# One two-layer hybrid block on one core: where the first output projection's bias is added, and when the convolution's taps are dealt

## Chip, cores and metric

The kernel runs on one core of one Trainium2 chip. The metric is the device time of one execution in microseconds (us), from launch to end on that core. Three executions of the kernel before gave 811.22, 810.73 and 818.46 us; the median is 811.22 us.

## What is computed

256 latent rows and 256 context rows of width 1024 go through two layers. Each layer has a mixer and a mixture of experts, and both are modulated by vectors that come from a conditioning input through a large matrix (`ada_w`, `ada_b`). The change touches the first layer's mixer only:

```python
m = jnp.split(silu_c @ ada_w[0] + ada_b[0], 6, axis=-1)          # one set for latent rows, one for context rows
u = h * (1 + m[1]) + m[0]
a, q, k, v = split(u @ w_in + b_in)
conv = silu(layer_norm(depthwise_conv(glu(a), conv_w, conv_b)))   # 31 taps, 512 channels
na   = attention(q, k, v)                                         # 8 heads; context rows and windowed latent rows
o    = concat([conv, na]) @ w_out + b_out
h    = layer_norm(alpha * h + m[2] * o)
```

So the row that is normalised is alpha·h + m2·(cat·w_out + b_out). After it come routing and the experts of layer 1, then the second layer.

## The kernel before

All weights stream from HBM through one list (`stream`) of 1 MB chunks. `pump` issues the next chunk on SyncE's queue (SP) whenever a buffer is free. There are four steady buffers (`w0` to `w3`); large scratch areas `x0` to `x4` are added to the free list by `lend` when the work that lives in them is over. The expert chunks of which the kernel knows the number ahead of routing are limited to 12 (`KNOWN0`). The order on every engine is the order in which the Python code emits instructions.

Products are made of three matmuls in float32r (`mm3`, lines 408 to 413): high part by high part, and the two mixed parts. Each weight chunk is therefore split into a high and a low part (lines 390 and 391, ScalarE and VectorE, or GpSimd where `low` is set; lines 401 and 402 do it piecewise on GpSimd during attention).

The stages of the first mixer, in order:

- `load_consts` (line 438 on): ScalarE's queue loads constants and, through `load_adab` (line 463), the modulation's bias: eight DMAs for each call, one for each of four column blocks and two conditioning vectors. `ada_done` (line 491) issues two more such calls on SP's queue.
- `inproj0` (line 581): ten chunks of the input projection. After each chunk some modulation matmuls (`self.ada(ADA_IN[c])`, line 482), then the evacuation of the chunk (lines 640, 641, 649, 651), then the split of a later chunk, then `self.bg(TAPS_IN[c])`. That last call emits convolution taps, which are VectorE instructions of 128x512 (line 632; the first of each channel block is line 630). There are 124 taps and four statistics steps in one queue, `bgq`.
- `attn0` (line 755) with `attend`: 32 jobs (a head and 128 query rows each) in a software pipeline over `i`. Scores on TensorE (line 786), maximum on VectorE (699), exponential on ScalarE (705), reciprocal on VectorE (713), scaling on GpSimd (714), transposes on TensorE (721), copy on ScalarE (723), product with v on TensorE (730), copies into the high and low operand of the next stage on ScalarE (577) and VectorE (578). A `hook(i)` after each step emits pieces of the output weight's split, `self.bg(TAPS_AT[i])`, the steps of the convolution's layer norm (`CONV_AT`), and modulation matmuls.
- `outproj` (line 861), called from `mix0` (line 2238): the output projection, four row tiles t of 128 rows, two column halves h of 512. First both weight groups of half 0 (`n` = 0, 1; attention rows first), into four PSUM banks `mm`; then half 1, tile by tile. There are four banks named `mm` in rotation. `end(t, h, ps)` multiplies a bank by m2 (line 2296, in `add_rows`), adds the residual row (line 878), and takes statistics (882); for h = 1 it also normalises the row. For layer 0 `forward` transposes the normalised row (569, 1126, 1128) and `back` computes routing logits (987) and transposes back through two more `mm` banks (1141).
- During `n` = 0 the hook in `mix0` emits the last four steps of the convolution's branch (lines 845 to 847, 574, 575), broadcasts m2 to all partitions (538, 533), multiplies it by the broadcast bias into `mb` (GpSimd, line 2273, four of 128x512) and turns the residual rows into alpha·x + mb (VectorE, line 2276, four of 128x1024). The bias row `bo` is loaded just before on ScalarE's queue (line 2253) into area 3, beside a zeroed tile that clears 4 MB in DRAM (line 2257).

Area 2 holds the attention's probabilities, area 3 the relative-position bias and later `bo` and the zeros, areas 0 and 1 the split of the last output weight, area 4 the convolution. Before, area 2 is lent at the end of `attn0`; areas 4 and 3 at `n` = 1, t = 0; areas 0 and 1 at the end.

Of the kernel before, what the change touches and what calls it, by code (L numbers as in the profile page):

```python
# [11 lines left out]
F32 = mybir.dt.float32  # L12
# [19 lines left out]

TAPS_IN = [9, 10, 10, 11, 12, 12, 12, 12, 14, 10]
TAPS_AT = [i % 2 for i in range(32)]

# [236 lines left out]
class Kern:  # L272
# [134 lines left out]

    def mm3(self, out, a, b, start, stop):
        (ah, al), (bh, bl) = a, b
        t = self.nc.tensor  # L410
        t.matmul(out, ah, bh, start=start, stop=False)  # L411
        t.matmul(out, ah, bl, start=False, stop=False)  # L412
        t.matmul(out, al, bh, start=False, stop=stop)  # L413

# [23 lines left out]
    def load_consts(self):  # L438
# [24 lines left out]
    def load_adab(self, l, g0, g1, at, eng):  # L463
        for j in range(4):
            src = self.d["ada_b"][l:l + 1].rearrange("o (g j n) -> o g j n", g=3, j=4)[:, g0:g1, j, :]
            for c in range(2):
                r = slice(32 * j + c, 32 * j + c + 1)
                if at == 4:
                    eng.dma_start(self.adar[4][r, :], src[:, 0])
                else:  # L470
                    eng.dma_start(self.adat[r, at:at + g1 - g0], src)

# [107 lines left out]

    def inproj0(self, M):
        nc, d, W = self.nc, self.d, self.W
# [171 lines left out]

    def attn0(self, M, qT, kT, v, acc):
        nc, d, W = self.nc, self.d, self.W
# [46 lines left out]
        def hook(i):  # L803
# [7 lines left out]
            if i % 2 == 1 and i // 2 < 16:  # L811
                self.ada(ADA_AT[i // 2])


# [40 lines left out]
        assert not self.bgq  # L855
        self.lend(self.end0 + 2, 2)

        return cath, catl, ln


    def outproj(self, l, cath, catl, tiles, order, base, hook=None):

        nc, T = self.nc, len(tiles)
        st, ends = {}, {}

        def prod(p, t, g, w, ks, start, stop):
            col = tiles[t][0]
            for k in ks:
                kt, sl = 4 * g + k, slice(k * 512, k * 512 + 512)
                self.mm3(p, (cath[:, kt, col:col + 128], catl[:, kt, col:col + 128]), (w[0][:, sl], w[1][:, sl]),  # L870
                         start and k == 0, stop and k == 3)

        def end(t, h, ps):
# [3 lines left out]
            yield  # L877
            nc.vector.tensor_tensor(s, s, o, op=OP.add)
            yield
# [1358 lines left out]
    def mix0(self):  # L2238
        nc, d, V = self.nc, self.d, self.nc.vector
        with self.phase("m0") as M:  # L2240
            with self.phase("m0i"):
                a = self.inproj0(M)
            with self.phase("m0a"):
                cath, catl, ln = self.attn0(M, *a)
# [4 lines left out]
                mb = M.tile([128, 4, 512], F32, name="v").rearrange("p (c h) n -> p c (h n)", c=2)  # L2249
                bo = self.area(3, [2, 1024])  # L2250
                bo, zero = bo[:, 0], bo[:, 1]
                nc.gpsimd.memset(zero, 0.0)
                nc.scalar.dma_start(bo, bass.AP(tensor=d["bo"].tensor, offset=d["bo"].offset, ap=[[0, 128], [1, 1024]]))

# [4 lines left out]
                def hook(n, t):  # L2259
                    if n == 0:  # L2260
                        next(ln)
                    if n == 1 and t == 0:
                        self.lend(self.end0, 4)
                        self.lend(self.end0 + 2, 3)
                    if n == 2 and t == 1:
                        self.ada_flush()
                    t -= 1
                    if n == 0 and t in (0, 1):
                        for h in range(2):
                            self.bcast_mod(m2[:, t], 1, 0, t, self.tp if h else None, halves=(h,))  # L2270
                        for h in range(2):
                            s = slice(h * 512, h * 512 + 512)
                            nc.gpsimd.tensor_tensor(mb[:, t, s], m2[:, t, s], bo[:, s], op=OP.mult)
                        for r in (2 * t, 2 * t + 1):
                            x = self.nt(r)
                            V.scalar_tensor_tensor(x, x, ALPHA, mb[:, t], op0=OP.mult, op1=OP.add)

                return self.outproj(0, cath, catl, TILES0, (1, 0, 0, 1),
                                    self.add_rows([m2[:, 0], m2[:, 1]], ("pT", 4)), hook)

# [286 lines left out]
```

## Time and profile before

| what | value |
|---|---|
| median of three runs | 811.22 us |
| the profiled execution's own time | 809.93 us |
| its span, first to last instruction | 808.1 us |
| TensorE busy (matmuls) | 711.7 us, 88% |
| VectorE busy | 475.1 us, 59% |
| ScalarE busy | 275.0 us, 34% |
| GpSimd busy | 236.8 us, 29% |
| mean granted TensorE clock | 0.944 |

How to read the rows below. A row of the timeline is: start, duration (us), engine, source line, operation, output <- input, shape, count; in brackets the idle time of that engine just before, and what released it. PE is TensorE, DVE VectorE, ACT ScalarE, POOL GpSimd; a q behind a name is that engine's queue of DMA issues. Rows of the same line in a row are merged, and the duration is then that of the whole run. A row of the windows view is: the stretch, its length, the busy time of PE, PEld (weight loads), DVE, ACT, POOL with counts, then the TensorE clock that was granted (1 is full), the busy share of the DMA engines, and GB/s. Busy shares are means over stages with different limits, so the argument goes by stage.

### The profile page before, as it was taken

How to read it: one execution, taken by the hardware profiler on the slowest of the kernel's cores; microseconds unless marked ns; L12 is line 12 of the kernel's file. 1: busy time of each engine (PE TensorE's matmuls, PEld its weight loads, DVE VectorE, ACT ScalarE, POOL GpSimd, SP SyncE). 2: the span in 40 equal slices, each digit the busy share in tenths (PEclk: the TensorE clock that was granted, in tenths of full speed). 3: DMA queues.
4: the chain of work that ended last, by engine and by line, in shares of the span. 5: the costliest groups of instructions: out<-in, count | busy, mean ns of one | idle time of the engine just before them, and what ended most of it. 6: DMA issues, size and time to landing. Idle time of an engine off the chain costs nothing. (4 is left out here: it accounts for less than half of the span.)

```text
span 808.1 us, 11464 instructions
## 1 busy us (share of the span) xinstructions
PE 711.7 (88%) x4162; PEld 417.9 (52%) x4162; DVE 475.1 (59%) x1004; ACT 275.0 (34%) x603; POOL 236.8 (29%) x254
## 2 busy tenths in 40 slices
PE   3799999949988987999999768969999987899993
PEld 0477777714566764434433337857556754454431
DVE  0578787866756878723334188397676388332115
ACT  0531222125756144201100127445677533121121
POOL 1200000026634012663000084163386450111111
PEclk9699999969999997999999978999999997899997
DMA  9974656447467528999997931637655494996892
GB/s 358 375 266 157 260 209 254 166 193 238 166 208 287 208 110 304 389 350 364 415 393 323 391 131 53 208 125 285 268 167 199 166 371 160 423 372 248 352 373 93
DMA packets 36269, 209.66 MB, mean 259 GB/s; under 512 B 4455, under 2 KB 4711, under 8 KB 15072
## 3 DMA queue, kind: packets, MB, share of 16 engines
q1 hardware_dynamic: 27872, 183.55, 58.8%
q10 hardware_dynamic: 4848, 13.86, 5.2%
q0 software_dynamic: 3472, 11.31, 3.7%
q8 instruction: 37, 0.61, 0.3%
q14 instruction: 40, 0.33, 0.1%
HBM read 197.92 MB, written 12.06 MB: 260 GB/s over the span
## 5 line engine op out<-in xcount | busy, mean ns | idle before, releaser
L632 DVE SCALAR_TENSOR_TENSOR x<-x,sm,x 128x512 f32<-128x512 f32 x120 | 90.7, 755 | 3.5
L411 PE MATMUL mm<-H,wh 128*128 128x512 f32 (+1 forms) x208 | 78.5, 377 | 1.8 <-ACT H L615 1.8
L413 PE MATMUL mm<-H,wl 128*128 128x512 f32 (+1 forms) x208 | 76.3, 367 | 0.7 <-DVE wl L391 0.7
L412 PE MATMUL mm<-L,wh 128*128 128x512 f32 (+1 forms) x208 | 76.5, 368 | 0.0
L482 PE MATMUL aux<-w,sc 128*32 128x512 f32 x368 | 52.2, 658 | 25.1 <-issue 9.2
L391 DVE TENSOR_TENSOR wl<-w,wh 128x512 fp32r<-128x512 f32 (+1 forms) x27 | 43.5, 1646 | 24.4 <-ACT wh L390 24.3
L401 POOL TENSOR_SCALAR wh<-w 128x256 fp32r<-128x256 f32 x32 | 13.7, 428 | 117.4 <-DMA w<-wo 117.3
L411 PEld LDWEIGHTS mm<-H,wh 128*128 128x128 f32 x208 | 40.3, 194 | 13.7 <-issue 2.5
L699 DVE TENSOR_REDUCE mx<-mm 128x1 f32<-128x512 f32 (+1 forms) x64 | 39.2, 616 | 13.2 <-PE mm L786 7.2
L1805 POOL TENSOR_TENSOR yl<-ada,yh 128x512 fp32r<-128x512 f32 x12 | 15.3, 1275 | 106.9 <-ACT yh L1802 106.9
L413 PEld LDWEIGHTS mm<-H,wl 128*128 128x128 f32 x208 | 40.3, 194 | 7.9 <-DVE wl L391 1.3
L412 PEld LDWEIGHTS mm<-L,wh 128*128 128x128 f32 x208 | 40.3, 194 | 7.1 <-DVE L L618 0.6
L411 PE MATMUL mm<-wh,H 128*128 128x512 f32 x104 | 42.8, 411 | 0.0
L723 ACT COPY pT<-tp 128x512 f32<-128x512 f32 (+1 forms) x64 | 33.9, 530 | 24.3 <-PE tp L721 24.0
L412 PE MATMUL mm<-wl,H 128*128 128x512 f32 x104 | 41.4, 398 | 0.0
L1382 PE MATMUL aux<-x,H 128*32 128x512 f32 (+2 forms) x104 | 37.9, 598 | 0.0
L1478 DVE TENSOR_TENSOR y<-mm,y 128x512 f32<-128x512 f32 x18 | 12.3, 690 | 42.8 <-PE mm L1400 42.7
L413 PE MATMUL mm<-wh,L 128*128 128x512 f32 x80 | 32.4, 405 | 2.6 <-DVE L L575 2.6
L390 ACT CAST wh<-w 128x512 fp32r<-128x512 f32 (+1 forms) x27 | 29.6, 1138 | 7.0 <-PE mm L413 6.9
L1799 DVE TENSOR_TENSOR ada<-pv,m 128x512 f32<-128x512 f32 x13 | 9.0, 692 | 39.0 <-PE pv L1400 39.0
L714 POOL TENSOR_SCALAR pexp<-pexp,ss 128x512 f32<-128x512 f32 x32 | 22.4, 700 | 31.7 <-DVE ss L713 22.2
L482 PEld LDWEIGHTS aux<-w,sc 128*32 128x32 f32 x368 | 8.5, 113 | 44.3 <-issue 20.1
(471 smaller groups left out, 1734.5 us busy)
## 6 DMA issues: line engine op xcount, KB each, us to landing
w<-ada_w SPq DMA_DIRECT2D x46, 1024.0 KB
x<-exp SPq DMA_DIRECT2D x35, 1024.0 KB
w<-exp SPq DMA_DIRECT2D x32, 1024.0 KB
w<-w SPq DMA_DIRECT2D x15, 1024.0 KB
wh<-exp SPq DMA_DIRECT2D x12, 1024.0 KB
wl<-exp SPq DMA_DIRECT2D x12, 1024.0 KB
w<-wo SPq DMA_DIRECT2D x8, 1024.0 KB
yd<-x ACTq DMA_DIRECT2D x1, 4096.0 KB
```

The costliest lines, as they stand in the source:

```text
L390: self.nc.scalar.copy(h[:, s], w[:, s])
L391: (self.nc.gpsimd if pool or low else self.nc.vector).tensor_tensor(l[:, s], w[:, s], h[:, s].bitcast(F32), op=OP.subtract)
L411: t.matmul(out, ah, bh, start=start, stop=False)
L412: t.matmul(out, ah, bl, start=False, stop=False)
L413: t.matmul(out, al, bh, start=False, stop=stop)
L482: nc.tensor.matmul(p[32 * j:32 * j + 32, :], self.sc[:, kt, :], w[:, j * 512:(j + 1) * 512], start=(kt == 0), stop=(kt == 7), skip_group_c ...
L632: nc.vector.scalar_tensor_tensor(acc[:, i], src, w, acc[:, i], op0=OP.mult, op1=OP.add)
L699: nc.vector.reduce_max(mx, p[:, :nk], axis=AX.X, negate=True)
L714: nc.gpsimd.tensor_scalar(P[i][:, :nk], P[i][:, :nk], r[:, 0:1], 0.0, op0=OP.mult, op1=OP.add)
L723: nc.scalar.copy(T[i][:, :nk], t[:, :nk])
L1382: self.nc.tensor.matmul(p[r], x(kt)[:, r], w_j[:, kt % 4 * 512:kt % 4 * 512 + 512], start=(kt == 0), stop=(kt == 7), skip_group_check=True)
L1805: (V if u == N - 1 else nc.gpsimd).tensor_tensor(lo, y, hi.bitcast(F32), op=OP.subtract)
```

## The change

Five edits, all of which act in layer 0:

1. The taps are dealt in another way. `TAPS_IN` goes from 9, 10, 10, 11, 12, 12, 12, 12, 14, 10 to 11, 12, 12, 12, 13, 13, 13, 13, 7, 2, and attention takes one tap in each of i = 1 to 9 (before in odd ones only).
2. The output projection's bias is loaded early, into area 1, and copied by ScalarE into the PSUM banks before the matmuls accumulate onto it: four banks of half 0 in the last steps of attention, and the banks of half 1 one tile ahead.
3. `mb`, its four multiplications and the four updates of the residual rows go away; line 878 becomes s·alpha + o for layer 0.
4. The areas change roles: the last output weight's split is in areas 0 and 2; area 3 is lent at `n` = 0, t = 0, area 4 at `n` = 1, t = 0, area 1 after the last bias copy, areas 0 and 2 at the end. Area 2 is no longer lent at the end of attention.
5. `load_adab` issues two DMAs of four partitions each (32 apart) in place of eight of one; one of its two calls at the start moves from ScalarE's queue to SP's, behind the loads of x.

```diff
-TAPS_IN = [9, 10, 10, 11, 12, 12, 12, 12, 14, 10]
-TAPS_AT = [i % 2 for i in range(32)]
+TAPS_IN = [11, 12, 12, 12, 13, 13, 13, 13, 7, 2]
+TAPS_AT = [int(i % 2 or 0 < i < 10) for i in range(32)]
...
-    def mm3(self, out, a, b, start, stop):
+    def mm3(self, out, a, b, start, stop, onto=False):
...
+        t.matmul(out, ah, bh, start=start, stop=False, skip_group_check=onto)
+        t.matmul(out, ah, bl, start=False, stop=False, skip_group_check=onto)
+        t.matmul(out, al, bh, start=False, stop=stop, skip_group_check=onto)
...
         self.load_adab(0, 0, 3, 0, nc.scalar)
-        self.load_adab(1, 1, 2, 3, nc.scalar)
...
     def load_adab(self, l, g0, g1, at, eng):
-        for j in range(4):
-            src = self.d["ada_b"][l:l + 1].rearrange("o (g j n) -> o g j n", g=3, j=4)[:, g0:g1, j, :]
-            for c in range(2):
-                r = slice(32 * j + c, 32 * j + c + 1)
+        src = self.d["ada_b"][l].rearrange("(g j n) -> j g n", g=3, j=4)[:, g0:g1]
+        for c in range(2):
+            r = slice(c, 128, 32)
...
             nc.sync.dma_start(xa[h // 2][:, h % 2 * 2:h % 2 * 2 + 2], d["xT"][:, 2 * h:2 * h + 2])
+        self.load_adab(1, 1, 2, 3, nc.sync)
...
                 nc.scalar.dma_start(self.rout, d["rout"])
+                nc.scalar.dma_start(bo, bass.AP(tensor=d["bo"].tensor, offset=d["bo"].offset, ap=[[0, 128], [1, 1024]]))
...
                 self.ada(ADA_AT[i // 2])
+            if i > 32:
+                banks.append(self.mm())
+                nc.scalar.copy(banks[-1], bo[:, 0:512])
...
-        self.lend(self.end0 + 2, 2)
...
-    def outproj(self, l, cath, catl, tiles, order, base, hook=None):
+    def outproj(self, l, cath, catl, tiles, order, base, hook=None, bias=None, banks=None):
...
+        def bank(h):
+            p = self.mm()
+            if bias is not None:
+                nc.scalar.copy(p, bias[:, h * 512:h * 512 + 512])
+            return p
...
-                         start and k == 0, stop and k == 3)
+                         bias is None and start and k == 0, stop and k == 3, bias is not None)
...
-            nc.vector.tensor_tensor(s, s, o, op=OP.add)
+            if l:
+                nc.vector.tensor_tensor(s, s, o, op=OP.add)
+            else:
+                nc.vector.scalar_tensor_tensor(s, s, ALPHA, o, op0=OP.mult, op1=OP.add)
...
-        p = [self.mm() for _ in range(T)]
+        p = banks or [bank(0) for _ in range(T)]
...
-                self.wq.append(self.split(bufs=[self.area(i, [2048], F32R) for i in (0, 1)], low=l == 0))
+                self.wq.append(self.split(bufs=[self.area(i, [2048], F32R) for i in ((0, 1) if l else (0, 2))], low=l == 0))
...
+        nxt = bank(1)
         for t in range(T):
-            p = self.mm()
+            p = nxt
             prod(p, t, order[2], w[0], range(4), True, False)
+            if t < T - 1:
+                nxt = bank(1)
+                if l == 0 and t == T - 2:
+                    self.lend(self.end0 + 2, 1)
             prod(p, t, order[3], w[1], range(2), False, False)
...
-        self.lend(len(self.stream) if l else self.end0 + 2, 0, 1)
+        self.lend(len(self.stream) if l else self.end0 + 2, 0, 1 if l else 2)
...
                 def hook(n, t):
                     if n == 0:
                         next(ln)
+                    if n == 0 and t == 0:
+                        self.lend(self.end0 + 2, 3)
                     if n == 1 and t == 0:
                         self.lend(self.end0, 4)
-                        self.lend(self.end0 + 2, 3)
...
                             self.bcast_mod(m2[:, t], 1, 0, t, self.tp if h else None, halves=(h,))
-                        for h in range(2):
-                            s = slice(h * 512, h * 512 + 512)
-                            nc.gpsimd.tensor_tensor(mb[:, t, s], m2[:, t, s], bo[:, s], op=OP.mult)
-                        for r in (2 * t, 2 * t + 1):
-                            x = self.nt(r)
-                            V.scalar_tensor_tensor(x, x, ALPHA, mb[:, t], op0=OP.mult, op1=OP.add)
```

More of the change, by code (lines that the diff above doesn't have):

```diff
@@ L406, in split_steps @@
             yield
-    def mm3(self, out, a, b, start, stop):
+    def mm3(self, out, a, b, start, stop, onto=False):
         (ah, al), (bh, bl) = a, b
         t = self.nc.tensor
-        t.matmul(out, ah, bh, start=start, stop=False)
-        t.matmul(out, ah, bl, start=False, stop=False)
-        t.matmul(out, al, bh, start=False, stop=stop)
+        t.matmul(out, ah, bh, start=start, stop=False, skip_group_check=onto)
+        t.matmul(out, ah, bl, start=False, stop=False, skip_group_check=onto)
+        t.matmul(out, al, bh, start=False, stop=stop, skip_group_check=onto)
     def mm(self):
@@ L463, in load_adab @@
     def load_adab(self, l, g0, g1, at, eng):
-        for j in range(4):
-            src = self.d["ada_b"][l:l + 1].rearrange("o (g j n) -> o g j n", g=3, j=4)[:, g0:g1, j, :]
-            for c in range(2):
-                r = slice(32 * j + c, 32 * j + c + 1)
[L468 to L471, printed above, removed]
+        src = self.d["ada_b"][l].rearrange("(g j n) -> j g n", g=3, j=4)[:, g0:g1]
+        for c in range(2):
+            r = slice(c, 128, 32)
+            if at == 4:
+                eng.dma_start(self.adar[4][r, :], src[:, 0])
+            else:
+                eng.dma_start(self.adat[r, at:at + g1 - g0], src)
     def ada_all(self):
@@ L578, in hl_from, with inproj0 @@
             self.nc.vector.scalar_tensor_tensor(l, src, bias, h.bitcast(F32), op0=OP.add, op1=OP.subtract)
-    def inproj0(self, M):
+    def inproj0(self, M, bo):
         nc, d, W = self.nc, self.d, self.W
@@ L753, in attend, with attn0 @@
             done()
-    def attn0(self, M, qT, kT, v, acc):
+    def attn0(self, M, bo, qT, kT, v, acc):
         nc, d, W = self.nc, self.d, self.W
@@ L812, in hook @@
                 self.ada(ADA_AT[i // 2])
+            if i > 32:
+                banks.append(self.mm())
+                nc.scalar.copy(banks[-1], bo[:, 0:512])
+        banks = []
         cbv = self.sm[:, 156:168].rearrange("p (s t) -> p s t", t=4)
@@ L855, in attn0 @@
         assert not self.bgq
-        self.lend(self.end0 + 2, 2)
-        return cath, catl, ln
-    def outproj(self, l, cath, catl, tiles, order, base, hook=None):
+        return cath, catl, ln, banks
+    def outproj(self, l, cath, catl, tiles, order, base, hook=None, bias=None, banks=None):
         nc, T = self.nc, len(tiles)
         st, ends = {}, {}
+        def bank(h):
[3 more added lines that the diff above has]
+            return p
         def prod(p, t, g, w, ks, start, stop):
@@ L877, in end @@
             yield
-            nc.vector.tensor_tensor(s, s, o, op=OP.add)
+            if l:
+                nc.vector.tensor_tensor(s, s, o, op=OP.add)
+            else:
+                nc.vector.scalar_tensor_tensor(s, s, ALPHA, o, op0=OP.mult, op1=OP.add)
             yield
@@ L2241, in mix0 @@
             with self.phase("m0i"):
-                a = self.inproj0(M)
+                bo = self.area(1, [1024])
+                a = self.inproj0(M, bo)
             with self.phase("m0a"):
-                cath, catl, ln = self.attn0(M, *a)
+                cath, catl, ln, banks = self.attn0(M, bo, *a)
                 self.nts = [self.C.tile([128, 2, 1024], F32, name=f"N{i}") for i in range(2)]
@@ L2248, in mix0 @@
                 m2 = M.tile([128, 4, 512], F32, name="qT").rearrange("p (c h) n -> p c (h n)", c=2)
-                mb = M.tile([128, 4, 512], F32, name="v").rearrange("p (c h) n -> p c (h n)", c=2)
-                bo = self.area(3, [2, 1024])
-                bo, zero = bo[:, 0], bo[:, 1]
+                zero = self.area(3, [1024])
                 nc.gpsimd.memset(zero, 0.0)
-                nc.scalar.dma_start(bo, bass.AP(tensor=d["bo"].tensor, offset=d["bo"].offset, ap=[[0, 128], [1, 1024]]))
                 self.yd = self.dram.tile([1024, 1024], F32, name="yd")
@@ L2270, in hook @@
                             self.bcast_mod(m2[:, t], 1, 0, t, self.tp if h else None, halves=(h,))
-                        for h in range(2):
-                            s = slice(h * 512, h * 512 + 512)
-                            nc.gpsimd.tensor_tensor(mb[:, t, s], m2[:, t, s], bo[:, s], op=OP.mult)
-                        for r in (2 * t, 2 * t + 1):
-                            x = self.nt(r)
-                            V.scalar_tensor_tensor(x, x, ALPHA, mb[:, t], op0=OP.mult, op1=OP.add)
                 return self.outproj(0, cath, catl, TILES0, (1, 0, 0, 1),
-                                    self.add_rows([m2[:, 0], m2[:, 1]], ("pT", 4)), hook)
+                                    self.add_rows([m2[:, 0], m2[:, 1]], ("pT", 4)), hook, bo, banks)
     def mix1(self):
```

## The prediction, made before the changed kernel ran

> **What bounds the kernel now.** I read the page's slices first: TensorE is at nine or ten tenths nearly everywhere in the first mixer, with dips at 160 to 180 and at 250 to 260 us. Then the windows view over these, then the timeline inside.
>
> ```profile
> 160.00:170.00 10.00, 3.39 (x26) 1.14 (x24) 7.52 (x11) 1.87 (x2) 0.00 (x0) 0.87 0.76 288
> 170.00:180.00 10.00, 6.50 (x26) 2.52 (x28) 5.66 (x18) 3.45 (x14) 4.31 (x7) 0.50 0.29 106
> 250.00:260.00 10.00, 7.37 (x32) 5.27 (x31) 9.07 (x7) 7.35 (x8) 5.68 (x4) 0.98 0.72 295
> 260.00:270.00 10.00, 10.00 (x39) 8.09 (x38) 9.86 (x8) 0.00 (x0) 3.47 (x1) 0.85 0.35 117
> 350.00:360.00 10.00, 10.00 (x66) 3.49 (x65) 3.00 (x4) 1.34 (x3) 5.96 (x5) 1.00 1.02 364
> ```
>
> At 160 to 170 TensorE works 3.39 of 10 us while VectorE works 7.52, and the granted clock falls to 0.50 after it. At 250 to 260 VectorE is at 9.07 and TensorE at 7.37. At 350 the experts run with the DMA engines full (1.02, 364 GB/s): later than that, time is won only if the weight stream moves along too.
>
> The first hole, in the timeline:
>
> ```profile
> 162.16 0.69 DVE L487 TENSOR_TENSOR adar<-aux,adar 128x512 f32<-128x512 f32 x1 [2.79 <-PE aux L482]
> 162.77 7.83 DVE L632 SCALAR_TENSOR_TENSOR x<-x,sm,x 128x512 f32<-128x512 f32 x10
> 170.66 0.75 DVE L699 TENSOR_REDUCE mx<-mm 128x1 f32<-128x256 f32 x2
> 172.52 0.17 DVE L506 COPY mods<-aux 128x16 f32<-128x16 f32 x1
> 162.91 0.66 PE L495 MATMUL aux<-cb,adar 128*128 128x128 f32 x4 [0.18 <-DVE adar L487]
> 172.78 1.93 PE L482 MATMUL aux<-w,sc 128*32 128x512 f32 x8 [9.22 <-issue]
> ```
>
> Ten taps (the last entry of `TAPS_IN`) stand on VectorE between line 487 and attention's first maxima. TensorE's next work (482) needs the bank that line 506 empties, and 506 stands behind taps and maxima: a hole of 9.22 us.
>
> The second hole:
>
> ```profile
> 250.93 4.54 DVE L2276 SCALAR_TENSOR_TENSOR N<-N,v 128x1024 f32<-128x1024 f32 x2 [5.03 <-POOL v L2273]
> 255.39 0.68 DVE L575 TENSOR_TENSOR L<-pT,H 128x512 fp32r<-128x512 f32 x1
> 255.99 2.35 DVE L2276 SCALAR_TENSOR_TENSOR N<-N,v 128x1024 f32<-128x1024 f32 x2
> 258.26 0.69 DVE L575 TENSOR_TENSOR L<-pT,H 128x512 fp32r<-128x512 f32 x1
> 258.86 6.76 DVE L391 TENSOR_TENSOR wl<-w,wh 128x2048 fp32r<-128x2048 f32 x1
> 258.70 4.77 POOL L391 TENSOR_TENSOR x<-w,x 128x2048 fp32r<-128x2048 f32 x1 [4.32 <-ACT x L390]
> 256.12 0.50 PE L413 MATMUL mm<-wh,L 128*128 128x512 f32 x1 [0.72 <-DVE L L575]
> 259.00 0.50 PE L413 MATMUL mm<-wh,L 128*128 128x512 f32 x1 [1.91 <-DVE L L575]
> ```
>
> The residual updates (2276), themselves late behind GpSimd's products, hold up the low halves of the convolution's rows (575); TensorE waits 0.72 + 1.91 us for these, and then runs at half clock.
>
> **Taps.** TensorE is full from 50 to 160 us, so the question is whether VectorE has room for 11 more taps there.
>
> ```profile
> 72.59 7.83 DVE L632 SCALAR_TENSOR_TENSOR x<-x,sm,x 128x512 f32<-128x512 f32 x10
> 80.97 0.75 DVE L641 SCALAR_TENSOR_TENSOR x<-mm,sm,x 128x512 f32<-128x512 f32 x1 [0.55 <-ACT x L640]
> 82.76 2.29 DVE L391 TENSOR_TENSOR wl<-w,wh 128x2048 fp32r<-128x2048 f32 x1 [1.03 <-ACT wh L390]
> ```
>
> Ten taps take 7.83, so one takes 0.78 us. A chunk has 0.55 + 1.03 = 1.58 us of idle; the two taps added to c = 2 are 1.57. It just fits, and line 391 works a chunk ahead, so some backlog would not reach TensorE: 0. If all of it went through, it would cost at most 11 · 0.78 = 8.6; I keep 0 to 1. At the far end eight taps less (10 to 2) stand ahead of the first maxima: 8 · 0.78 = 6.3 us, and line 487 before them stays where it is, since TensorE releases it. The hole shrinks to 9.22 − 6.3 = 2.9 us. Term: −6.3.
>
> The four extra taps of attention (3.1 us of VectorE) go into 166 to 185, where VectorE is 5.66 of 10 busy and waits for scores. There the reciprocals come a little later, but GpSimd reaches its scaling later still: +0.2, bounds 0 and 3.1, near the lower because of the idle.
>
> **The clock.** With edges at 259.57 plus multiples of 3.41 us the granted clock changes on edges:
>
> ```profile
> 256.16:259.57 3.41, 1.50 (x6) 0.93 (x6) 3.41 (x4) 3.39 (x3) 0.87 (x1) 1.00 0.26 106
> 259.57:262.98 3.41, 3.41 (x10) 2.64 (x9) 3.41 (x1) 0.35 (x1) 3.41 (x1) 0.50 0.02 5
> 532.64:536.05 3.41, 1.55 (x11) 1.50 (x12) 3.21 (x8) 1.74 (x5) 0.93 (x2) 1.00 1.01 420
> 536.05:539.46 3.41, 2.88 (x25) 1.85 (x23) 2.88 (x5) 3.24 (x7) 2.43 (x2) 1.00 0.25 103
> ```
>
> A window with 1.50 us of work is followed by half clock, one with 1.55 is not. So about 1.9 us of idle inside one window is enough. A hole of 2.9 us with an edge at random puts 1.9 into one window about three times in four. I therefore keep the slow start of attention; no gain from the clock there.
>
> The Trainium skill, "TensorE: Matmul & The Clock Gate", Part 1, says that the clock is halved after an idle window of about 3.4 us; by that a hole of 2.9 us would leave it whole, which is the rival "warm" below. The trace speaks against it: the window with 1.50 us of work was not idle.
>
> **Out-projection.** Lines 2273 and 2276 go: four products on GpSimd, and 4.54 + 2.35 = 6.9 us of VectorE. Line 575 then follows ScalarE at once, and TensorE loses neither the 2.63 us nor the window at half clock (3.41 · 0.5 = 1.7): −4.3 by TensorE alone. Against it, the four bank copies at the end of attention:
>
> ```profile
> 234.80 0.37 ACT L577 ACTIVATE H<-pv,sm 128x128 fp32r<-128x128 f32 x1
> 235.38 0.59 ACT L723 COPY pT<-tp 128x512 f32<-128x512 f32 x1 [0.21 <-PE tp L721]
> 235.78 1.33 PE L730 MATMUL pv<-pT,v 128*64 128x128 f32 x16 [0.49 <-DVE L L578]
> 245.56 0.59 ACT L533 COPY qT<-tp 128x512 f32<-128x512 f32 x1
> ```
>
> A copy of 128x512 takes ScalarE 0.59 (533 reads PSUM; a copy into it is not in the trace; from a third of that to twice it would be 0.2 to 1.2). The first one stands ahead of 577 and 723, for which the last products of attention wait: +0.45. The other three run beside TensorE.
>
> But half 1 doesn't follow TensorE alone:
>
> ```profile
> 256.73 1.89 ACT L390 CAST x<-w 128x2048 fp32r<-128x2048 f32 x1
> 265.54 0.68 DVE L2296 TENSOR_TENSOR pT<-mm,qT 128x512 f32<-128x512 f32 x1
> 267.60 0.67 DVE L2296 TENSOR_TENSOR pT<-mm,qT 128x512 f32<-128x512 f32 x1
> 274.90 0.69 DVE L2296 TENSOR_TENSOR pT<-mm,qT 128x512 f32<-128x512 f32 x1 [0.72 <-PE mm L413]
> 279.07 1.09 PE L569 MATMUL tp<-cb,N 128*128 128x128 f32 x8
> ```
>
> VectorE works off half 0 from 265.54 to 274.18 (8.64 us), and TensorE's transposes of the first finished row come 279.07 − 274.90 = 4.17 after half 1's first product. When does that chain begin? Above, VectorE's 391 started at 258.86 beside GpSimd's and took 6.76 in place of 2.29, ending 2.1 us after GpSimd's: it did nothing until GpSimd was through. After the change VectorE's split comes first (ScalarE's first cast, 0.45 later than before, ends near 257.3, the split at 259.6), GpSimd's starts then, and its 4.77 last until 264.4. The new line 878 has two operands in SBUF, like 391 and 2276, and waits. Whether 2296, with one operand in PSUM, may run in that time, no row here shows; I take it that it may (0.7 later if not). So the chain goes on at 264.4: as if begun at 263.7, plus 8.64 and four times 0.07 for the dearer form (755 ns for 512 columns in the group below, against 0.68 for line 2296), to 272.6; transposes at 276.8. Gain 2.3, not 3.9.
>
> ```profile
> L632 DVE SCALAR_TENSOR_TENSOR x<-x,sm,x 128x512 f32<-128x512 f32 x120 | 90.7, 755 | 3.5
> ```
>
> TensorE, there at 275.2 or a little sooner, waits about 1.6 to 2.1 us, near the limit for the clock: 0.3 · 1.7 = +0.5. Term: −2.3 + 0.5.
>
> The Trainium skill, "SBUF — State Buffer", section "Who interferes with whom", calls this an exclusive lock, held for a whole instruction, between GpSimd and a VectorE instruction with two SBUF inputs; one with a single SBUF input takes no part. By that line 2296 runs and the 0.7 is not paid; no row here shows it.
>
> Half 1's banks: copies of 0.59 one tile ahead; they wait only for a bank that line 2296 has read long before. The rotation changes, though:
>
> ```profile
> 290.40 0.69 DVE L2296 TENSOR_TENSOR pT<-mm,qT 128x512 f32<-128x512 f32 x1 [0.46 <-PE mm L413]
> 290.91 0.66 PE L1141 MATMUL mm<-cb,wh 128*128 128x128 f32 x4
> ```
>
> At t = 2 the transposes of `back` now get the bank that line 2296 is reading; they start at 291.1 at the soonest rather than at 290.91: +0.25.
>
> **The areas.** Before:
>
> ```profile
> 235.37 0.33 SPq L323 DMA_DIRECT2D x<-exp  x1
> 266.55 33.03 SPq L323 DMA_DIRECT2D x<-exp  x4
> ```
>
> Three expert chunks (x2; x4, x3) came ahead of the out-projection's end, two (x0, x1) at it. After: x3 (behind the clear of area 3), x4, x1 ahead, x0 and x2 at the end. Three and two again: 0. A chunk is 1.05 MB / 364 GB/s = 2.9 us, which is the price if one is late. Since the rest of the stream starts when the out-projection and routing end, it moves with them.
>
> **Bias loads.** 14 issues fewer on ScalarE's queue at the start, where TensorE waits for the modulation's weights, and 10 fewer on SP's, most of them in the in-projection, where TensorE is full: 0; I keep 0.5 either way for the first chunks.
>
> **Sum.** −6.3 + 0.2 − 2.3 + 0.5 + 0.25 = −7.65 (the 0.45 is inside the −2.3). The execution took 809.93 (its span and 1.83 around it), so 802.3; the median lies 1.29 above it: 803.6.
>
> **Rivals.**
> - "Warm": the clock stays whole over the hole of 2.9 us. For: one time in four by the edges. The clock was 0.50 in all of 170 to 180, so some 7 us of work from 172.8 on could have taken 3.5; less 0.5 for VectorE's extra taps, which then weigh: −3.0, 800.6.
> - "No lock": line 878 runs beside GpSimd's split; half 1 follows TensorE. For: two of 2276 got through in 4.54 us beside GpSimd's products. Against: alone two took 2.35. −3.9 for −2.3, no wait and so no 0.5: 801.5.
> - "Not in time": the copies lag, TensorE waits for one at each of half 1's four banks, 4 · 0.6: 806.0. Against: ScalarE has no work from 260 to 270.
> - Slower, "stream": the weights set the end of layer 1, and their start doesn't move. x3 waits for the 4 MB clear and blocks SP's queue, x1 comes after the end of half 1. From the point where two chunks are missing when the experts begin, nothing of the gain comes through and 2 · 2.9 is added: 817. For: DMA at 1.02 at 350. Against: 266.55's issues wait for buffers, not for bandwidth, and the DMA engines are at 0.35 at 260 to 270.
>
> **Chances.** Forecast 0.55, warm 0.17, no lock 0.15, not in time 0.07, stream 0.06. 1% is 8.1 us, about what a measurement of this kernel can tell from no change, and below 803.1 would be faster by more. The forecast at 803.6 with some 1.5 either way lies below that four times in ten (0.22), warm and no lock nearly always (0.26 together): faster 0.48, same 0.46, slower 0.06. The range reaches from both favourable rivals together, 798.5, to a case with three more bounds gone wrong, 808.5.
>
> **What would show it.** Right: ten taps become two after line 487, the hole before 482 near 3 us; no idle before 413 in the out-projection; VectorE's 391 near 2.3 us, its new 878 waiting for GpSimd's split; transposes 569 some 8.5 us sooner than 279.07, and all after it by as much. Wrong: VectorE late at 391 in the in-projection, matmuls waiting for ScalarE's bank copies, or the experts' stage starting with fewer chunks.

## The result, and the profile after

The changed kernel takes 801.99 us (median of 4 runs, 800.67 to 802.09). Beside it on that chip the kernel before took 811.73 (4 runs): ratio 0.9847, 95% interval 0.9808 to 0.9886. The two profiled executions took 802.09 and 809.93 us: 7.84 us less. The forecast was 803.6.

In the changed kernel most lines have moved by a few: 480, 485, 493, 504, 573, 567, 631, 893 and 2309 are the 482, 487, 495, 506, 575, 569, 632, 878 and 2296 of before; the bank copies are lines 816 and 875. First the windows of the kernel after, over the stretches that the prediction showed of before:

```profile
160.00:170.00 10.00, 6.76 (x46) 2.52 (x45) 5.00 (x14) 3.55 (x9) 1.42 (x2) 1.00 0.79 294
170.00:180.00 10.00, 7.62 (x49) 3.34 (x50) 6.61 (x19) 4.74 (x17) 7.60 (x12) 0.83 0.54 188
250.00:260.00 10.00, 10.00 (x45) 8.20 (x44) 8.79 (x6) 3.68 (x4) 4.87 (x1) 1.00 0.73 232
260.00:270.00 10.00, 8.67 (x39) 6.83 (x38) 8.75 (x19) 2.99 (x5) 0.00 (x0) 1.00 0.45 190
```

TensorE (the first busy time) has 6.76 of 10 us in place of 3.39 at 160, and no gap at 250; the clock (the third column from the end) is 0.83 in place of 0.50 at 170 and 1.00 in place of 0.85 at 260. The first hole in its timeline:

```profile
162.84 0.69 DVE L485 TENSOR_TENSOR adar<-aux,adar 128x512 f32<-128x512 f32 x1 [7.88 <-PE aux L480]
163.44 1.53 DVE L631 SCALAR_TENSOR_TENSOR x<-x,sm,x 128x512 f32<-128x512 f32 x2
165.03 0.75 DVE L699 TENSOR_REDUCE mx<-mm 128x1 f32<-128x256 f32 x2
166.89 0.16 DVE L504 COPY mods<-aux 128x16 f32<-128x16 f32 x1
167.15 1.07 PE L480 MATMUL aux<-w,sc 128*32 128x512 f32 x8 [2.91 <-issue]
172.81 0.69 PE L721 MATMUL tp<-cb,x 128*128 128x128 f32 x2 [1.95 <-POOL x L714]
```

Two taps stand where ten stood, and the hole is 2.91 us, where the prediction had 2.9. The out-projection:

```profile
251.11 2.29 DVE L391 TENSOR_TENSOR wl<-w,wh 128x2048 fp32r<-128x2048 f32 x1 [1.12 <-ACT wh L390]
253.32 0.68 DVE L2309 TENSOR_TENSOR pT<-mm,qT 128x512 f32<-128x512 f32 x1
254.04 4.41 DVE L893 SCALAR_TENSOR_TENSOR N<-N,pT 128x512 f32<-128x512 f32 x1
253.03 4.87 POOL L391 TENSOR_TENSOR x<-w,x 128x2048 fp32r<-128x2048 f32 x1 [24.69 <-ACT x L390]
269.75 1.09 PE L567 MATMUL tp<-cb,N 128*128 128x128 f32 x8 [1.33 <-ACT N L907]
```

VectorE's split runs in its own 2.29 us (6.76 before). The new update, line 893, takes 4.41 us and ends 0.55 after GpSimd's split; line 2309 before it, with an operand in PSUM, ran in 0.68 beside the same split. Below, "the lock" is short for this: a VectorE instruction with both operands in SBUF and GpSimd's split do not run side by side, and the one that comes second waits. No row shows TensorE waiting for low halves any more. The transposes of the first finished row come at 269.75 in place of 279.07.

To see where the time went in this and all later runs, I cut each profiled execution at five marks: A, the modulation's transposes (495 of before) near 163 us; B, the first scores 512 wide (786); C, the out-projection's first product (411); D, the transposes of the first finished row (569); E, the broadcast of the modulation's rows for the experts (the first `mm<-adar,one`). The columns are A's time and the lengths between marks, and from E to the end of the span.

| kernel | profiled, us | A | A–B | B–C | C–D | D–E | E–end |
|---|---|---|---|---|---|---|---|
| before | 809.93 | 162.91 | 34.70 | 39.43 | 42.03 | 33.46 | 495.6 |
| before, second profile | 815.16 | 163.31 | 33.88 | 39.44 | 47.92 | 33.47 | 495.4 |
| after | 802.09 | 163.58 | 27.16 | 40.62 | 38.39 | 33.60 | 497.0 |
| after, second profile | 801.83 | 162.99 | 29.83 | 39.65 | 38.42 | 33.55 | 495.6 |
| taps alone | 811.54 | 164.05 | 28.33 | 39.43 | 48.43 | 33.53 | 495.9 |
| bias loads alone | 811.75 | 162.42 | 33.86 | 39.42 | 43.42 | 33.55 | 497.2 |
| out-projection alone | 805.64 | 162.70 | 32.36 | 40.64 | 38.47 | 33.53 | 496.1 |
| taps alone, split in quarters | 808.76 | 164.34 | 27.19 | 40.64 | 45.47 | 33.56 | 495.7 |
| before, split on VectorE | 812.38 | 164.92 | 34.71 | 39.45 | 42.23 | 33.47 | 495.7 |
| after, split in quarters | 799.56 | 163.08 | 29.62 | 39.64 | 37.21 | 32.90 | 495.2 |
| after, other dealing | 797.48 | 162.80 | 27.04 | 39.62 | 38.47 | 32.86 | 494.8 |
| after, banks laid late | 804.61 | 163.58 | 28.30 | 42.69 | 41.10 | 32.81 | 494.3 |
| both improvements | 798.84 | 162.67 | 24.35 | 40.60 | 37.21 | 33.06 | 499.1 |
| both, extra taps late | 796.59 | 162.47 | 24.77 | 42.64 | 37.18 | 32.79 | 494.9 |

After against before, first profiles: A +0.67, A to C −6.35, C to D −3.64, D to E +0.14, E to the end +1.35, in all −7.8. The last term is not the change's: in the second profile of the same kernel it is gone. One thing that differs there is a wait of TensorE for rows that the experts gather, in the first profile and in the second:

```profile
327.40 1.06 PE L567 MATMUL tp<-cb,xg 128*128 128x128 f32 x8 [2.95 <-DMA xg<-td,ridx]
326.38 1.06 PE L567 MATMUL tp<-cb,xg 128*128 128x128 f32 x8 [0.47 <-DMA xg<-td,ridx]
```

### The profile page after: what moved, and what is told of

Read it like the earlier page. It is cut to its first block, busy times and chain, and to the rows that moved or that the text cites. A ratio compares the mean times of both kernels' runs of the same rounds, so it can differ in the third digit from the quotient of the medians.

```text
span 800.3 us, 11447 instructions
## 1 busy us (share of the span) xinstructions
PE 710.1 (89%) x4162; PEld 416.7 (52%) x4162; DVE 466.5 (58%) x1000; ACT 279.4 (35%) x611; POOL 233.5 (29%) x250
## 5 line engine op out<-in xcount | busy, mean ns | idle before, releaser
L391 DVE TENSOR_TENSOR wl<-w,wh 128x512 fp32r<-128x512 f32 (+1 forms) x27 | 39.8, 1511 | 20.8 <-ACT wh L390 20.6
L411 PEld LDWEIGHTS mm<-H,wh 128*128 128x128 f32 x208 | 40.6, 195 | 14.0 <-issue 3.4
L412 PEld LDWEIGHTS mm<-L,wh 128*128 128x128 f32 x208 | 40.6, 195 | 7.0 <-DVE L L617 0.4
L412 PE MATMUL mm<-wl,H 128*128 128x512 f32 x104 | 40.6, 390 | 0.0
L1402 PE MATMUL pv<-w,X 128*32 128x512 f32 (+2 forms) x96 | 30.1, 596 | 0.0
```

Of the source, the lines that this page charges most:

```text
L391: (self.nc.gpsimd if pool or low else self.nc.vector).tensor_tensor(l[:, s], w[:, s], h[:, s].bitcast(F32), op=OP.subtract)
L411: t.matmul(out, ah, bh, start=start, stop=False, skip_group_check=onto)
L412: t.matmul(out, ah, bl, start=False, stop=False, skip_group_check=onto)
L1402: self.nc.tensor.matmul(p[r], x(kt)[:, r], w_j[:, kt % 4 * 512:kt % 4 * 512 + 512], start=(kt == 0), stop=(kt == 7), skip_group_check=True)
```

## The experiments

All times below are medians against the kernel before on the same chip, which there took 814.8 to 816.0 us, not 811.7.

**Taps alone**: the kernel before with the new `TAPS_IN` and `TAPS_AT`.

> The kernel before with the two new lists of taps and nothing else. Theory (the taps are most of the gain, through the hole before the modulation's matmuls and the clock after it): the hole of 9.22 us shrinks to about 2.9, the first 512-wide scores of attention start near 190.7 in place of 197.61 (-6.9), out-projection still shows both waits for the low halves, the first transposes of a finished row come at 279.07 - 6.9 = 272.2, and the time is 811.7 - 6.9 = 804.8. The prediction's own term for this part was -6.1 (805.6). Rival 1 (the slow clock stays and only part of the hole is won): 808. Rival 2 (the extra taps in the in-projection cost 3 us or more, seen as a later start of the chunk at 137 us): 808 or more.

Measured 808.58 us (ratio 0.9935, 0.9901 to 0.9969). Up to C the theory held: hole 2.92 us, A to C 6.4 us shorter. Then the out-projection gave it back, transposes at 280.24 in place of the expected 272.2. Its timeline:

```profile
253.77 4.98 DVE L575 TENSOR_TENSOR L<-pT,H 128x512 fp32r<-128x512 f32 x1
253.48 4.72 POOL L391 TENSOR_TENSOR x<-w,x 128x2048 fp32r<-128x2048 f32 x1 [3.58 <-ACT x L390]
258.80 0.79 PE L413 MATMUL mm<-wh,L 128*128 128x512 f32 x1 [6.20 <-DVE L L575]
```

GpSimd's split began 0.3 us ahead of VectorE's last low half, which took 4.98 us in place of 0.69 and ended 0.55 after the split. In the first profile of before line 575 began at 258.26 and the split at 258.70: the other order. The twelve runs lie between 805.03 and 813.11, and three of them at 805.0 to 805.7, near the 804.8 of the theory; that these three had the other order is likely, but no profile shows it.

**Bias loads alone.**

```diff
-        for j in range(4):
-            src = self.d["ada_b"][l:l + 1].rearrange("o (g j n) -> o g j n", g=3, j=4)[:, g0:g1, j, :]
...
+        src = self.d["ada_b"][l].rearrange("(g j n) -> j g n", g=3, j=4)[:, g0:g1]
```

> The kernel before with the four strided loads of the modulation's bias and nothing else. Theory: the first matmul comes 0.6 us sooner (29.7 in place of 30.29), the in-projection takes that back by 60 us since it is bound further on by the weights and by VectorE, and the time stays at 811.7 within 0.6. Rival: the 0.6 us goes through to the end: 811.1, with every marker after 60 us sooner by 0.6.

Measured 811.38 us (0.9974, 0.9938 to 1.0009), not told from no change. The first product of the in-projection came 0.54 us sooner (29.75), and over all fourteen profiles it comes at 29.57 to 30.00 with the new loads, at 30.08 to 32.29 with the old. A came 0.49 sooner, so 60 us did not take it back here; but A scatters by more than that, from 162.70 to 164.92 in the four profiles with the old taps and the old loads.

In this profile VectorE's last low half (line 573 here) and GpSimd's split are almost tied:

```profile
257.29 0.68 DVE L573 TENSOR_TENSOR L<-pT,H 128x512 fp32r<-128x512 f32 x1
257.32 5.17 POOL L391 TENSOR_TENSOR x<-w,x 128x2048 fp32r<-128x2048 f32 x1 [3.90 <-ACT x L390]
```

VectorE began 0.03 us ahead and took 0.68 us.

**Out-projection alone**: the kernel after with the old taps and loads.

> The kernel after with the old lists of taps and the old loads of the modulation's bias: the out-projection's part of the change alone. Theory (GpSimd's split keeps VectorE's new update waiting, so that only part of TensorE's 4.3 us comes through): the update waits some 3.7 us beyond its 0.69, the first transposes of a finished row come at 276.6 (-2.5), the time is 809.3. The prediction had -1.6 with its terms of the clock and the bank. Rival 1, no lock: 275.1 and 807.8. Rival 2, the copies into the banks cost attention's end nothing (what was lost there, some 1.2 us, was the clock's phase): out-projection starts at 237.0 as before, and the transposes come at 275.4.

Measured 805.60 us (0.9900, 0.9850 to 0.9949), with 4.41 us for the update again, as the theory had it, but 3.7 us under the theory's 809.3. C to D is 38.47, 3.56 less than in the first profile of before; D, at 274.17, is 2.4 sooner than expected, partly because A to C took 1.1 us less than before with the same taps. B to C is 40.64 here; the run with the banks laid late shows what that means.

**GpSimd's split in four pieces**, in the kernel after.

```diff
-                self.wq.append(self.split(bufs=[self.area(i, [2048], F32R) for i in ((0, 1) if l else (0, 2))], low=l == 0))
+                self.wq.append(self.split(bufs=[self.area(i, [2048], F32R) for i in ((0, 1) if l else (0, 2))], low=l == 0, n=1 if l else 4))
```

> The kernel after with GpSimd's split of the out-projection's last weights cut into four pieces of 512 columns (and ScalarE's cast of it too). Theory (the one long GpSimd instruction holds the lock, and VectorE can step in between two short ones): the update that took 4.41 us takes 2 us or less, VectorE's work on the first half ends 2 to 3.7 us sooner than 265.6, TensorE's idle 1.33 us before the transposes of the first finished row goes, and these come at 268.4 to 268.9 in place of 269.75; the time is 801 (-1.0 to -1.3 on 802.0). Rival 1 (the update waited for something else, such as its operand from the PSUM bank, or VectorE shares a port evenly with GpSimd): 4.4 us or the same sum over two instructions, transposes at 269.75, 802.0. Rival 2 (what is won here is swallowed by the weights' stream or the gathers at the start of the experts): transposes 1.3 us sooner, the experts' steps after 327 us not, 802.0.

Measured 800.24 us (0.9832, 0.9784 to 0.9880).

```profile
255.08 1.07 DVE L893 SCALAR_TENSOR_TENSOR N<-N,pT 128x512 f32<-128x512 f32 x1
257.51 1.62 DVE L893 SCALAR_TENSOR_TENSOR N<-N,pT 128x512 f32<-128x512 f32 x1
252.78 7.51 POOL L391 TENSOR_TENSOR x<-w,x 128x512 fp32r<-128x512 f32 x4 [22.47 <-ACT x L390]
```

The waiting falls from 3.72 to 0.38 + 0.93 us, TensorE's idle 1.33 us is gone and C to D is 37.21, 1.18 shorter, as the lock has it. D comes only 0.20 us sooner since C came 0.98 later (the clock, below). The time alone does not show the gain: its interval overlaps that of the kernel after (0.9808 to 0.9886).

**The kernel after once more**, for its time on the same chip and a second profile.

> The kernel after, unchanged, for its time on the same chip as the three others and for a second profile. Theory (the lost 1 to 3 us of the clock after the hole of 2.9 us depend on where the clock's window of 3.41 us falls in it): the hole is 2.91 to 2.92 us again, the matmuls after it run at full or at half clock by chance (1.07 or 1.94 us for eight), and out-projection starts within 1.5 us of 231.36; the update beside GpSimd's split waits again and takes 4.4 us. Time 800 to 803. Rival (the kernel's parts are repeatable to 0.3 us and the first profile is typical): full clock again, 231.4.

Measured 802.11 us (801.83 to 802.45; 0.9844, 0.9795 to 0.9894).

```profile
166.56 1.94 PE L480 MATMUL aux<-w,sc 128*32 128x512 f32 x8 [2.92 <-issue]
```

The same hole, but half clock behind it (1.94 us for eight matmuls; 1.07 in the first profile), and C 1.11 us later: the rival, that one profile is typical, is out.

**Other dealing of the taps**, in the kernel after.

```diff
-TAPS_IN = [11, 12, 12, 12, 13, 13, 13, 13, 7, 2]
+TAPS_IN = [11, 12, 12, 12, 12, 12, 12, 12, 13, 0]
```

> The kernel after with its taps dealt otherwise within the in-projection: 11, 12, 12, 12, 12, 12, 12, 12, 13, 0 (108 as before), so that no tap stands ahead of attention's first maxima and the chunks at 100 to 140 us have one less. Theory: the hole at 121.5 us falls from 1.20 to about 0.4 us, the hole before the modulation's matmuls from 2.91 to 1.35 us, too short for the clock, so that the matmuls after it run at full clock always; out-projection starts 2.3 us sooner and up to 3.5 with the clock, at 228 to 229 in place of 231.36; time 799. Rival 1 (the maxima wait for the scores or for the bias copies on GpSimd, not for the taps): the hole stays above 2 us and little is won, 801.5. Rival 2 (13 taps in the chunk at 140 us keep TensorE waiting for VectorE's low halves): nothing won, 802.

Measured 797.70 us (0.9786, 0.9733 to 0.9839).

```profile
120.71 1.92 PE L480 MATMUL aux<-w,sc 128*32 128x512 f32 x16 [0.42 <-PE aux L493]
164.92 1.66 PE L480 MATMUL aux<-w,sc 128*32 128x512 f32 x8 [1.47 <-issue]
171.70 0.44 PE L721 MATMUL tp<-cb,x 128*128 128x128 f32 x2 [1.95 <-POOL x L714]
173.12 1.94 PE L480 MATMUL aux<-w,sc 128*32 128x512 f32 x8
```

Both holes shrink as expected, and C comes at 229.46. But the clock still fell twice (1.66 and 1.94 in place of 1.07): "too short for the clock" was wrong. It goes by the execution here too: in the two later kernels with this dealing the hole is 1.46 and 1.47 us, and the eight matmuls take 1.06. The 1.95 us before line 721 is not the taps of the in-projection.

**Banks laid at the out-projection's start**: the three lines under `if i > 32` left out.

> The kernel after with the four banks of the out-projection's first half laid by ScalarE at the out-projection's start in place of the end of attention. Theory (these copies, 0.59 to 1.11 us each on ScalarE ahead of what attention's last products wait for, cost its end 1.2 us): from the first 512-wide scores to the out-projection's first product it takes 39.4 us as in the kernel before, in place of 40.6; the out-projection then waits 0.6 to 1.2 us for its first bank; the time is the same within 0.6: 802. Rival 1 (the end of attention lost to the clock's phase, the copies are free): 40.6 still, and the out-projection waits as well: 803. Rival 2 (the first bank is laid in a gap and nothing waits): 800.8.

Measured 805.46 us (0.9888, 0.9836 to 0.9940).

```profile
230.03 1.33 PE L730 MATMUL pv<-pT,v 128*64 128x128 f32 x16 [0.49 <-DVE L L576]
234.57 0.79 PE L411 MATMUL mm<-wh,H 128*128 128x512 f32 x1 [3.22 <-ACT mm L871]
```

The last products of attention end 39.5 us after B (231.36 − 191.88), with the copies it is 39.6 or 40.6. The table and the windows show what the two values are. 40.64 also stands in the run with taps and quarters, which has no bank copies; and from B to C the granted clock is 1.00 in all eight profiles that took 39.42 to 39.65 and 0.96 in all four that took 40.60 to 40.64. At full clock it takes 39.42 to 39.45 without the copies and 39.62 to 39.65 with them. So the copies cost about 0.2 us, the other 1.0 is the clock; my theory of 1.2 for the copies fell (the 1.11 us that it gives for one copy is the time of two). The late banks cost 3.22 us, not 0.6 to 1.2: on ScalarE's queue they stand behind the four issues of `xtok` (1.78 us) and one of `yd`.

**Taps alone, and the split in quarters.**

> The kernel before with the new lists of taps and with GpSimd's split of the out-projection's last weights cut into four pieces of 512 columns. Theory (with the new lists alone the taps' gain was lost again because GpSimd's split, one instruction of 4.72 us, took the lock ahead of VectorE's low half of the convolution's last rows, which took 4.98 us in place of 0.69, and TensorE waited 6.20 us): that low half takes 2 us or less, TensorE's wait falls from 6.20 to 2.5 or less, the transposes of the first finished row come at 274.5 to 276.5 in place of 280.24, and the time is 804 in place of 808.6. Rival (the low half is late because the bias rows and the residual rows come late by DMA, and the lock is only what fills the time): the wait stays at 5 us or more, 808.6.

Measured 808.59 us (0.9933, 0.9907 to 0.9960), the same as taps alone.

```profile
251.59 3.43 DVE L2276 SCALAR_TENSOR_TENSOR N<-N,v 128x1024 f32<-128x1024 f32 x2
254.94 1.74 DVE L575 TENSOR_TENSOR L<-pT,H 128x512 fp32r<-128x512 f32 x1
256.74 0.79 PE L413 MATMUL mm<-wh,L 128*128 128x512 f32 x1 [4.05 <-DVE L L575]
```

The low half is under 2 us and the wait 2.15 less, but not 2.5: the pieces now also hold up the residual updates ahead of it (3.43 for 2.35). D comes 2.6 us sooner than in the profile of taps alone; the medians don't show it. What is missing there stays open.

**Before, with the split on VectorE**: `low=False` in place of `low=l == 0`.

> The kernel before with one thing changed: the low halves of the out-projection's last weights are made by VectorE, not by GpSimd, so that GpSimd has no long instruction while VectorE makes the low halves of the convolution's rows. Theory (it is a race in the kernel before: whether GpSimd's split or VectorE's last low half takes the lock first makes the out-projection's first half short or long, 42.03 us from the first product to the first transposes in one profile, 48.43 in another of the same instructions, and this spreads the runs of before from 807 to 819 us): the last low half takes 0.69 us, TensorE's second wait is 1.9 to 2.5 us, 39.5 to 41 us from first product to first transposes, the runs lie within 6 us and their median is 808 to 810, some 5 us under that of before on this chip. Rival (the spread of before comes from the clock's phase or from elsewhere; two splits in a row on VectorE cost 2.3 us): median 815 and the spread stays at 10 us or more.

Measured 812.16 us (0.9956, 0.9932 to 0.9981), ten runs from 808.05 to 813.24; the kernel before beside it from 809.56 to 817.56.

```profile
260.52 0.68 DVE L575 TENSOR_TENSOR L<-pT,H 128x512 fp32r<-128x512 f32 x1
261.25 0.50 PE L413 MATMUL mm<-wh,L 128*128 128x512 f32 x1 [1.90 <-DVE L L575]
```

No lock and a wait of 1.90 us as expected; no run above 813.3. But C to D is 42.23, that of the short outcome, and not the 39.5 to 41 expected, and the median I had put 2 to 4 us too low. The runs still spread over 5.2 us without the race, so the race is not all of the spread.

**Before, a second profile.**

> The kernel before, unchanged, for a second profile (its first one took 809.93 us where the median of 23 runs on another chip was 814.8). Theory (its out-projection has two outcomes, by which of GpSimd's split and VectorE's last low half takes the lock first; the first profile was the short one): from the out-projection's first product to the first transposes 46 to 48.5 us in place of 42.03, the last low half 3 to 5 us long in place of 0.69, TensorE's second wait 4 to 6.5 us in place of 1.91, and the time 813 to 817; or the short outcome again with a time near 810. Rival (the stage always takes 42 us and the spread of the runs is elsewhere): 42 us with a time of 813 or more.

The profiled execution took 815.16 us, and it is the long outcome:

```profile
258.74 4.98 DVE L575 TENSOR_TENSOR L<-pT,H 128x512 fp32r<-128x512 f32 x1
258.22 4.95 POOL L391 TENSOR_TENSOR x<-w,x 128x2048 fp32r<-128x2048 f32 x1 [3.36 <-ACT x L390]
263.77 0.80 PE L413 MATMUL mm<-wh,L 128*128 128x512 f32 x1 [6.21 <-DVE L L575]
```

C to D is 47.92 us, 5.89 more than in the first profile, and all other stages agree within 0.9: the whole difference of 5.23 us is this place. In the four profiles that have the old out-projection and GpSimd's long split, the order goes with the outcome: VectorE began 0.44 and 0.03 us ahead of the split where C to D took 42.03 and 43.42, and 0.29 and 0.52 behind it where it took 48.43 and 47.92. The eight runs lie at 809.4 to 811.9 (four) and 813.3 to 816.7 (four). Their median, 812.57, stands at a ratio of 0.9948 (0.9914 to 0.9982) to the very same instructions beside them. So a ratio within half a per cent of 1 says nothing where a kernel has the old out-projection: the times of taps alone, taps with quarters and split on VectorE are not told from before by themselves; their profiles are.

**Both improvements**: other dealing and quarters. **And with the extra taps of attention late**: `17 < i < 25` in place of `0 < i < 10`.

> The kernel after with the other dealing of the taps (none ahead of attention's first maxima) and with GpSimd's split in four pieces. Theory (the two gains lie in different stages and add up: the dealing gave 797.7 for 802.1, the pieces 1.2 us of the out-projection's first half): 37.2 us from the out-projection's first product to the first transposes, these at 266.7, time 796.4. Rival (the weights' stream sets the start of the experts and swallows the second gain): transposes at 266.7 and the time still 797.7.

> The same as the kernel with both, and the four extra taps of attention moved from its steps 2 to 8 to its steps 18 to 24. Theory (the taps between the first maxima make GpSimd's scaling late, and TensorE waits 1.95 us for it at 172 us and then runs at half clock): that wait falls to 0.7 us or less, and from the first transposes of the modulation's rows (162.8) to the first 512-wide scores it takes 24.5 to 26 us in place of 27.0; the later stage has room for them (VectorE 21 of 30 us busy), so the time is 794.5 to 795.5 in place of 796.4. Rival 1 (the later stage has no room: its chain from scores to product passes through VectorE): 39.6 us from these scores to the out-projection grow to 41 or more, and nothing is won, 796.4 or later. Rival 2 (the wait for GpSimd's scaling comes from GpSimd's own splits): it stays at 1.9 us.

Measured 796.59 us (0.9764, 0.9738 to 0.9791) and 796.22 (0.9762, 0.9731 to 0.9793). In the stages the two improvements stand together: the hole is 1.46 us and C to D 37.21. The times do not show the second one, since the interval lies within that of the other dealing alone (0.9733 to 0.9839). In the profile with both, D comes 3.1 us sooner than with the dealing alone, but 2.7 of this lie between A and B, where the granted clock was 1.00 in place of 0.87 with the same taps. From E to the end it then takes 4.3 us more. Part of that is the wait for gathered rows, 0.67 us with the dealing alone:

```profile
321.26 1.07 PE L567 MATMUL tp<-cb,xg 128*128 128x128 f32 x8 [2.04 <-DMA xg<-td,ridx]
```

So the rival, that the start of the experts can swallow a gain, is not out. The late taps give nothing: the wait of 1.95 falls to 1.51 only,

```profile
169.40 0.44 PE L721 MATMUL tp<-cb,x 128*128 128x128 f32 x2 [1.51 <-POOL x L714]
```

and B to C grows from 40.60 to 42.64 at the same granted clock of 0.96, as the first rival has it. The two times do not tell these two kernels apart.

## Why the prediction was right, and where it was wrong

The time was right, and the two mechanisms that carry it, the taps ahead of the maxima and the wait for the lock, were the right ones. Several smaller terms were mis-sized, and one choice about the time before was wrong.

That the sum of −7.65 came so close to the −7.84 between the two profiled executions is in part luck. The prediction makes A to C −5.65 (with the 0.45 of the bank copies), C to D −2.75 and D to E +0.75; the first profile has −6.35, −3.64 and +0.14, 2.2 us better in all. Against this stand +0.67 up to A and +1.35 from E on, which the prediction had at nothing; in the second profile these two are 0.1 or less, and A to C is −4.65.

- *Taps, −6.3 + 0.2.* Right in size: the hole is 2.91 to 2.92 in six profiles with these lists, and A to C is 4.7 to 6.4 us shorter than 74.13 in the five of them that lay the banks early or have none to lay. But "it just fits: 0" for the in-projection was too kind. There the copies of line 504 stand behind more taps, and the bank comes free later:

```profile
117.33 3.90 DVE L631 SCALAR_TENSOR_TENSOR x<-x,sm,x 128x512 f32<-128x512 f32 x5
121.14 0.25 DVE L504 COPY mods<-aux 128x16 f32<-128x16 f32 x2
121.49 1.92 PE L480 MATMUL aux<-w,sc 128*32 128x512 f32 x16 [1.20 <-issue]
```

  Before, the hole at this place was 0.41. That is 0.8 us; the other dealing took it away again. I had asked whether line 391 is late, and not who else waits behind a tap.
- *Clock at attention's start: no gain kept.* No rule held here. In the six profiles with this hole the eight matmuls behind it took 1.06 to 1.07 us, full clock, in four and 1.94, half clock, in two, where I had put half clock at three in four. In the first profile the clock fell 5 us later, so "warm" held there from 167 to 172 us only. One to three us hang on it: in the two profiles of the kernel after, A to B is 27.16 at a granted clock of 0.94 and 29.83 at 0.83, B to C 40.62 at 0.96 and 39.65 at 1.00.
- *Bank copies, +0.45.* Some 0.2.
- *Out-projection, −2.3 + 0.5.* The mechanism was right in each step: 391 at 2.29, the update waiting for GpSimd's split, line 2309 not waiting, transposes held by VectorE's chain (TensorE idle 1.33 us, 1.6 to 2.1 predicted). From C on the prediction makes it −2.75, measured −3.64: counted from C, GpSimd's split began 0.4 sooner than I had it, and the chain behind it took 7.7 us and not 8.2 (the new form costs 0.69, not 0.75). The 0.5 for the clock, counted behind D, was not paid. By the Trainium skill, "SBUF — State Buffer", "Who interferes with whom", a VectorE instruction with at most one SBUF input does not contend with GpSimd; the trace agrees (line 2309, with its other operand in PSUM, took 0.68 us inside GpSimd's 4.87).
- *Bank rotation, +0.25.* Not there: line 1161, 1141 of before, starts 0.50 us after line 2309 as it did.
- *Areas, stream: 0.* E to the end is 495.6 in the second profile, as before; its scatter over all profiles, 494.3 to 499.1, is in part the wait for gathered rows.
- *Bias loads: 0, with 0.5 either way.* They bring the first product about 0.5 us sooner.
- *The step that was wrong: "1.29 above".* I took the profiled execution of before as typical and carried its distance to the median over to the changed kernel. It was not typical: its out-projection was the short outcome of the race at line 575 (42.03 us from C to D), and another execution of the same program took 47.92. The change removes that race, and the changed kernel shows no such distance: its two profiled executions took 802.09 and 801.83 us, the medians are 801.99 and 802.11, and the eight runs lie within 1.8 us. Without the 1.29 the forecast is 802.3, within 0.4 of both medians. That the 1.29 itself came from the race is not shown: 811.22 also lies among the four low runs of before (809.4 to 811.9). So the gain is 7.8 us against the short outcome and some 13 against the long one (815.16). The rows that could have warned me were quoted: 575 at 258.26 and GpSimd's split at 258.70, 0.44 us apart.

## What to carry to other kernels

When two engines reach for the same lock within half a microsecond, a profile shows one of two kernels: work out the other order as well, and look for its time among the runs. Cut a long GpSimd instruction into pieces (four pieces took 7.51 us in place of 4.87 here, so it has a price), or let the VectorE work beside it read one operand from PSUM. When work is dealt onto an engine that "has room", list every short instruction that will stand behind it, not only the one with the slack; and compare stage by stage between marks, since 1 to 3 us move with the clock between executions of one program.

## What the runs showed of the hardware

The clock does not go by busy time alone. Windows of the kernel after, on edges 3.41 us apart (172.50 is one), some left out between (the clock is the third column from the end):

```profile
162.27:165.68 3.41, 1.79 (x16) 0.72 (x8) 2.81 (x6) 1.03 (x2) 0.00 (x0) 1.00 0.95 356
165.68:169.09 3.41, 1.94 (x14) 0.69 (x14) 1.28 (x6) 0.81 (x4) 0.89 (x1) 1.00 1.02 430
169.09:172.50 3.41, 1.20 (x8) 0.50 (x6) 3.41 (x10) 2.27 (x8) 2.94 (x4) 0.99 0.88 305
172.50:175.91 3.41, 3.10 (x18) 1.21 (x18) 1.31 (x4) 1.21 (x4) 2.80 (x5) 0.51 0.14 53
...
223.65:227.06 3.41, 1.78 (x17) 1.20 (x17) 1.60 (x7) 3.39 (x8) 2.20 (x5) 0.99 0.39 96
227.06:230.47 3.41, 3.30 (x24) 2.24 (x20) 2.21 (x6) 2.65 (x7) 1.28 (x2) 0.51 0.58 238
```

1.79 us of matmul work is followed by full clock at 165.68, 1.78 by half clock at 227.06, although the prediction's rows had 1.55 as enough. In the second profile a window at half clock that was busy for 3.01 of 3.41 us is followed by half clock again:

```profile
173.22:176.63 3.41, 3.01 (x18) 1.22 (x18) 1.40 (x4) 1.21 (x4) 2.88 (x5) 0.50 0.07 24
176.63:180.04 3.41, 3.41 (x18) 1.90 (x16) 1.61 (x6) 1.00 (x5) 0.94 (x2) 0.50 0.50 137
```

What is counted in a window stays open; edges 3.41 us apart fit all of these rows. The Trainium skill, "TensorE: Matmul & The Clock Gate", Part 1, asks for an idle window; none of these was idle, so here the trace differs.
